# Hybrid attention encoder on one core: attention units started at other places, a second direct weight group, four buffers for weight parts

## Chip, core and metric

The kernel runs on one core of one Trainium2 chip. TensorE (PE) multiplies, VectorE (DVE) and ScalarE (ACT) do the elementwise work, GpSimd (POOL) takes a little of it, and SyncE (SP) issues all transfers. The metric is the device time of one execution in microseconds (us); less is better.

## What is computed

One layer of an encoder is applied to two requests with the same weights: a prompt of 512 tokens and a sample of 1,024 tokens, 1,024 channels each, in float32.

```python
h = rms_norm(x, g_norm)
u = h @ w_in                                   # 1024 x 9728
qa, ka, va, za, qb, kb, vb, zb, qc, kc, vc, zc, gl = jnp.split(u, offs, axis=-1)
ya = neighborhood_attention(qa, ka, va, rpb)   # 8 heads, 8 x 16 window on a grid 64 wide
yb = diff_attention(qb, kb, vb, lam, ...)      # 4 heads, two softmax maps over all keys
yc = dilated_attention(qc, kc, vc, ...)        # 3 groups x 4 heads, windows 128/512/2048
pa = (ya * silu(za)) @ w_br_a                  # pb and pc likewise
merged = gates[:, :, 0] * pa + gates[:, :, 1] * pb + gates[:, :, 2] * pc
y = rms_norm(x + merged @ w_out, g_final)
```

## The kernel before

**Projection.** `w_in` has 9,728 columns, taken 256 at a time: 38 slots for the prompt, then 38 for the sample. A pair of 128 columns is multiplied by the Strassen scheme in `strassen`: seven products of half the inner length instead of eight. Weights and activations are each split into a high part in the fast float32 form and a low part, and a product is three runs of matmuls (`mm3`): high by high, low by high (`wl`), and bfloat16 by low (`wb`). `split_w` makes `wh`, `wl` and `wb` of one weight tile on ACT, DVE and POOL. A prompt matmul has 256 columns, a sample matmul 512. With `direct` the pair is multiplied without sums of weights (`ws`), by eight products. Before the change that holds for the first prompt slot alone (`DIRECT = 1`). Three slots of each request are taken double ("quads", `strassen_v`), for the values.

**Attention units.** Each request has 12 units: four differential heads (`mixer_b`), two pairs of a dilated unit and a window unit (`dilated`, `mixer_c`), and four neighbourhood units (`mixer_a`). All 24 run inside the sample's 38 slots: the prompt's while the first slots are multiplied, the sample's after that. `P_AT` and `S_AT` say at which slot each unit starts; it is spread evenly to the start of the next. A unit begins with a head: it fetches q and k and splits them into high and low halves (`qk<-stg`). A sample unit of `mixer_b` then has 32 softmax rows: one DVE instruction that takes a 128 x 512 tile of scores `s`, adds the distance term in `tab` and finds the maximum. The exponential follows on ACT, a scaled subtraction of the two maps on DVE, transposes on PE with a high and a low copy (`pt`, `pl`), and the product with the values (`o`).

**Order.** Nothing runs by program order alone. Each operation is recorded with a price and its predecessors, and a list scheduler (`Program.order`) decides once, at build time, in which order each engine's instructions stand and which buffer each tile gets. On the chip an engine takes its instructions strictly in that order. `CAPS` limits how many tiles of a name may be alive: `wh` 3, `wl` 2, `wb` 3 before. Operations with two possible engines go to the one that the planner finds less loaded. The priority is the order of recording, so a unit's head goes ahead of later projection work.

**End.** After slot 37 the branch projections and gates follow (`merge`, first prompt, then sample), and the output projection with the last norm (`output`).

The lines that the change touches are the tables after line 500, `CAPS`, and the `direct` branch of `strassen`. Slots are started in this loop:

```python
starts = P_AT + S_AT + [38]
...
        while j < len(units) and slot > starts[j]:
            unit, n = units[j]
            want = int(min(1, (slot - starts[j]) / (starts[j + 1] - starts[j])) * n + 1e-6)
```

Of the kernel before, what the change touches and what calls it, by code (L numbers as in the profile page):

```python
# [8 lines left out]
F32 = mybir.dt.float32  # L9
# [136 lines left out]
class Program:  # L146
# [323 lines left out]
    def emit(self, pools, static_pool, dram_pool):  # L470
# [29 lines left out]


HS_AT = 10
DIRECT = 1
QUADS_P = [2, 5, 8]
QUADS_S = [0, 2, 5]
P_AT = [1.0, 2.25, 3.0, 4.25, 5.0, 6.0, 7.25, 7.75, 8.2, 10.0, 12.25, 13.5]
P_ORDER = [0, 1, 2, 3, 4, 5, 6, 7, 8, 9, 10, 11]
S_AT = [14.2, 17.0, 19.0, 21.0, 23.5, 26.5, 27.0, 27.75, 31.0, 33.0, 34.0, 35.5]
S_ORDER = [0, 1, 2, 3, 4, 5, 6, 7, 8, 9, 11, 10]

SLOTS = {"k9": (2, 9216), "k8": (11, 8192), "k4": (18, 4096), "k2": (18, 2048), "k1": (3, 1024), "b": (8, 2048)}
CAPS = {"tab": ("k9", 2), "x": ("k9", 1), "ybl": ("k9", 1), "tpl": ("k9", 1),
# [7 lines left out]
for _t, (_n, _w) in {"rstd": (2, 1), "ss": (2, 1), "ss2": (3, 2), "st": (4, 4), "cz": (4, 2), "stb": (4, 6),  # L520
                     "czb": (2, 12), "st2": (2, 32), "s2n": (2, 32), "st1": (2, 32), "cmb": (1, 96),
                     "ff": (1, 32)}.items():
    SLOTS["s_" + _t] = (_n, 4 * _w)
    CAPS[_t] = ("s_" + _t, _n)
# [5 lines left out]
def build(ctx, tc, a):  # L530
    nc = tc.nc
    pg = Program(tc, nc, SLOTS, CAPS)
    act, dve, pool, pe = pg.act, pg.dve, pg.pool, pg.pe
# [15 lines left out]
    def copy(dst, src, scale=None, engines="AD"):  # L549

        ways = []
        if "A" in engines:
            ways.append((act, "activation", (dst, src, AF.Copy), {} if scale is None else {"scale": scale}))
        if "D" in engines and scale is None:
            ways.append((dve, "tensor_copy", (dst, src), {}))
        elif "D" in engines:
            ways.append((dve, "tensor_scalar", (dst, src, scale, None), {"op0": OP.mult}))
        pg.any(*ways)
# [73 lines left out]
    def put(dst, src, t):  # L632

        c = slice(128 * t, 128 * t + 128)
        hi, lo = dst
        if isinstance(lo, list):
            for i in range(2):
                split(hi[:, 2 * i:2 * i + 2, c], lo[i][:, :, c], src[:, 2 * i:2 * i + 2])
        else:
            split(hi[:, :, c], lo[:, :, c], src)  # L640
# [94 lines left out]
    def split_w(raw, half=True):  # L735

        n = raw.ap.ap[1][1]
        wh = pg.tile("wh", [128, 4, 128], F32R)[:, :n]
        wl = pg.tile("wl", [128, 4, 128], F32R)[:, :n]
        split(wh, wl, raw)  # L740
        ws = [wh, wl, wh]
        if half:
            ws[2] = pg.tile("wb", [128, 4, 128], BF16)[:, :n]
            copy(ws[2], raw)
        return [[w[:, k] for k in range(n)] for w in ws]

    def mm3(ps, w, xh, xl, first=True):

        n = len(xh)
        kw = {} if first else {"skip_group_check": True}  # L750
        for k in range(n):
            pe.matmul(ps, w[0][k], xh[k], start=first and k == 0, stop=False, **kw)
        for k in range(n):
            pe.matmul(ps, w[1][k], xh[k], start=False, stop=False, **kw)
        for k in range(n):
            pe.matmul(ps, w[2][k], xl[k], start=False, stop=k == n - 1, **kw)

    def strassen(raw, T, n, put, direct=False, early=None):

        a0, a1 = (raw[k][:, :, :128] for k in range(2))  # L760
        b0, b1 = (raw[k][:, :, 128:] for k in range(2))
        if direct:
            for i, (w0, w1) in enumerate(((a0, a1), (b0, b1))):
                w = [x + y for x, y in zip(split_w(w0), split_w(w1))]
                c = pg.tile("c", [128, 512], F32)
                for j in range(2):
                    ps = pg.tile("p", [128, 512], F32)[:, :n]
                    mm3(ps, w, *[[T[f"b{k // 4}{j}"][x][:, k % 4] for k in range(8)] for x in range(2)])
                    copy(c[:, n * j:n * j + n], ps)
                put(i, 0, c)  # L770
                yield
            return

        def ws(x, y, op):
# [813 lines left out]
    T = next(part)  # L1588
# [30 lines left out]
    def slots(s, T):  # L1619

        def make(i):
            quad = i in quads[s]

            def go():
                ahead(s, i + 1 + quad)
                if quad:
                    return project_v(s, cols[s][i], raws[s, i], T)
                return project(s, cols[s][i], raws[s, i], T, s == "p" and i < DIRECT)
            return Pair(not quad and not (s == "p" and i < DIRECT), go)
        return chain([None if c is None else make(i) for i, c in enumerate(cols[s])])  # L1630
# [19 lines left out]
    units = mixers("p", 512, P_ORDER) + mixers("s", 1024, S_ORDER)  # L1650
    starts = P_AT + S_AT + [38]
    ahead("s", 0)
    j = done = slot = 0
    for i, k in slots("s", TS):
        slot = i + k / 7
        while j < len(units) and slot > starts[j]:
            unit, n = units[j]
# [6 lines left out]
            j, done = j + 1, 0  # L1664
# [44 lines left out]
```

## Time and profile before

| what | value |
|---|---|
| median of 3 runs | 1871.55 us (1870.59 to 1872.54) |
| the profiled execution, its own time | 1870.9 us |
| its span, first to last instruction | 1869.1 us |
| mean granted TensorE clock | 0.995 |
| busy: PE / PE weight loads / DVE / ACT / POOL | 97 / 78 / 81 / 65 / 18 % |
| prompt slots end, sample slots end | about 415 us, about 1573 us |

Busy is the time in which an engine executed something. Matmuls are pipelined and each record covers its whole passage, so two that overlap leave no gap: a PE that is shown busy need not be at its peak, and waits shorter than a passage (about 0.3 to 0.4 us) do not show as idle time. The two times at the end are read from the first matmul that stands behind the last prompt slot's and the last sample slot's.

### The profile page before, as it was taken

The numbers are of one execution on the slowest core, as the hardware profiler recorded it, in microseconds if no ns is written. First come the engines' busy times: TensorE is split into PE (matmuls) and PEld (weight loads), VectorE is DVE, ScalarE is ACT, GpSimd is POOL, SyncE is SP. The second block draws the span as 40 slices with busy tenths as digits, with TensorE's granted clock in tenths as the row PEclk, the third lists the DMA queues.
The fourth block names the chain that finished last, engine by engine and source line by source line (L and its number), as shares of the span: only waits on it lengthen the run. The fifth ranks groups of instructions, "written<-read, shape, count | busy, mean of one in ns | idle before, by whom it ended". The sixth has DMA issues, their size and how long they took to land.

```text
span 1869.1 us, 32390 instructions
## 1 busy us (share of the span) xinstructions
PE 1811.9 (97%) x11343; PEld 1465.9 (78%) x11436; DVE 1515.3 (81%) x3061; ACT 1217.8 (65%) x2432; POOL 345.0 (18%) x296
## 2 busy tenths in 40 slices
PE   6999999999999999999999999999999999999998
PEld 6999999999989777778777787767777776666776
DVE  8879999997995786788999988578588886866665
ACT  6677878885675665666565657487587776633453
POOL 0000000000000000000000001000001144988874
PEclk9999999999999999999999999999999999999999
DMA  7645555553334454542122325246354557978541
GB/s 230 178 129 192 165 163 175 164 180 124 122 116 144 140 155 148 172 134 95 64 91 74 100 82 162 76 139 181 121 166 143 158 147 260 326 239 255 200 167 68
DMA packets 242336, 287.14 MB, mean 154 GB/s; under 512 B 33182, under 2 KB 168574, under 8 KB 242174
## 3 DMA queue, kind: packets, MB, share of 16 engines
q1 hardware_dynamic: 242174, 285.08, 48.2%
q8 instruction: 90, 1.47, 0.3%
q14 instruction: 72, 0.59, 0.1%
HBM read 203.93 MB, written 81.44 MB: 153 GB/s over the span
## 4 chain that ended last, share of the span: by engine, by line
PE 86%; DVE 6%; ACT 3%; DMA 2%; issue 1%; SPq 1%; POOL 0%; DVEq 0%; POOLq 0%; ACTq 0%
PE p L486 60%; PE s L486 15%; PE o L486 6%; PE t L486 6%; DVE qk L486 2%; SPq L486 1%; ACT qk L486 1%; DVE e L486 1%; DVE tab L486 1%; DMA rawq<-w_in 1%; ACT wh L486 0%; ACT c L486 0%; DVE wl L486 0%; POOL ybl L486 0%; DMA YG<-y 0%
## 5 line engine op out<-in xcount | busy, mean ns | idle before, releaser
L486 PE MATMUL p<-th,wh 128*128 128x512 f32 x1400 | 424.4, 414 | 2.9 <-ACT c L486 2.1
L486 PEld LDWEIGHTS p<-th,wh 128*128 128x128 f32 x1400 | 252.8, 189 | 58.5 <-issue 5.0
L486 PE MATMUL p<-th,wl 128*128 128x512 f32 x1016 | 295.6, 401 | 0.6 <-DVE wl L486 0.6
L486 ACT ACTIVATE wb<-raw 128x512 bf16<-128x512 f32 (+1 forms) x254 | 154.9, 614 | 177.5 <-PE p L486 99.7
L486 ACT ACTIVATE c<-p 128x512 f32<-128x512 f32 (+1 forms) x302 | 150.7, 500 | 111.5 <-PE p L486 104.5
L486 PEld LDWEIGHTS p<-th,wl 128*128 128x128 f32 x1016 | 186.7, 189 | 39.8 <-issue 2.4
L486 PE MATMUL s<-qk 128*128 128x512 f32 (+5 forms) x736 | 191.4, 363 | 7.1 <-DVE qk L486 4.0
L486 DVE TENSOR_TENSOR c<-p,c 128x512 f32<-128x512 f32 (+1 forms) x222 | 126.0, 576 | 84.0 <-PE p L486 44.8
L486 PEld LDWEIGHTS <-wb 128*128 128x128 bf16 x1376 | 107.6, 98 | 109.5 <-issue 50.1
L486 DVE CUSTOM_DVE_ANT_0 e<-s,tab 128x384 f32<-128x384 f32 (+3 forms) x256 | 129.7, 532 | 75.1 <-PE s L486 66.8
L486 DVE TENSOR_TENSOR wl<-ws,wh 128x512 fp32r<-128x512 f32 x252 | 172.9, 690 | 4.5 <-PE p L486 1.7
L486 ACT ACTIVATE pt<-t 128x512 fp32r<-128x512 f32 (+4 forms) x198 | 102.8, 537 | 96.3 <-PE t L486 93.5
L486 PE MATMUL p<-tp,wh 128*128 128x256 f32 x892 | 151.7, 295 | 4.5 <-ACT wh L486 3.7
L486 ACT ACTIVATE wh<-ws 128x512 fp32r<-128x512 f32 x239 | 148.0, 621 | 8.3 <-DVE ws L486 7.5
L486 PE MATMUL p<-tl,wb 128*128 128x512 bf16 x529 | 145.6, 381 | 4.4 <-issue 0.3
L486 PEld LDWEIGHTS s<-qk 128*128 128x128 f32 (+1 forms) x736 | 123.7, 189 | 31.9 <-issue 9.0
L486 ACT ACTIVATE wh<-raw 128x512 fp32r<-128x512 f32 (+1 forms) x224 | 134.5, 606 | 21.1 <-PE p L486 12.9
L486 PE MATMUL p<-tp,wl 128*128 128x256 f32 x892 | 145.2, 285 | 0.4 <-DVE rstd L486 0.2
L486 DVE TENSOR_TENSOR wl<-raw,wh 128x512 fp32r<-128x512 f32 (+1 forms) x201 | 140.6, 704 | 6.0 <-ACT wh L486 4.0
L486 POOL MEMSET qk<- 64x512 f32 (+1 forms) x48 | 37.2, 774 | 563.9 <-PE t L486 152.3
L486 ACT ACTIVATE e<-e,st 128x384 f32<-128x384 f32 (+2 forms) x192 | 105.2, 550 | 39.6 <-DVE st L486 39.1
L486 PE MATMUL p<-wq,th 128*128 128x256 f32 x816 | 128.4, 294 | 0.0
(230 smaller groups left out, 3773.8 us busy)
## 6 DMA issues: line engine op xcount, KB each, us to landing
raw<-w_in SPq DMA_DIRECT2D x140, 512.0 KB
Us<-c SPq DMA_DIRECT2D x128, 256.0 KB
Up<-c SPq DMA_DIRECT2D x64, 256.0 KB
stg<-Us SPq DMA_DIRECT2D x30, 512.0 KB
g<-Us SPq DMA_DIRECT2D x48, 256.0 KB
tab<-E SPq DMA_DIRECT2D x192, 48.0 KB
stp<-Up SPq DMA_DIRECT2D x30, 256.0 KB
YG<-y SPq DMA_DIRECT2D x30, 256.0 KB
```

The source lines that it names most:

```text
L486: getattr(engs[o.eng], o.meth)(*[val(x) for x in o.args], **{k: val(x) for k, x in o.kw.items()})
```

## The change

Four things: the second prompt slot is multiplied directly too; a direct pair is now gone through by token half first (both column blocks on the first half, then both on the second), with its result stored as soon as its second half is there; up to four tiles of `wh`, `wl` and `wb` may be alive; and the starts of the attention units are others. Of the tables the sample's is shown. The prompt's first five units started at 1.0, 2.25, 3.0, 4.25 and 5.0 and now start at 1.0, 2.4, 3.8, 5.2 and 6.6; the rest follow at distances of 0.8 to 1.0, where they were 0.45 to 2.25.

```diff
-DIRECT = 1
+DIRECT = 2
...
-S_AT = [14.2, 17.0, 19.0, 21.0, 23.5, 26.5, 27.0, 27.75, 31.0, 33.0, 34.0, 35.5]
+S_AT = [14.2, 17.3, 20.4, 23.5, 26.6, 28.2, 29.2, 30.8, 31.8, 33.3, 34.8, 36.3]
...
-SLOTS = {"k9": (2, 9216), "k8": (11, 8192), "k4": (18, 4096), "k2": (18, 2048), "k1": (3, 1024), "b": (8, 2048)}
+SLOTS = {"k9": (2, 9216), "k8": (11, 8192), "k4": (18, 4096), "k2": (18, 2048), "k1": (4, 1024), "b": (8, 2048)}
...
-        "tpb": ("k2", 6), "ws": ("k2", 4), "wh": ("k2", 3), "wl": ("k2", 2), "c": ("k2", 7),
+        "tpb": ("k2", 6), "ws": ("k2", 4), "wh": ("k2", 4), "wl": ("k2", 4), "c": ("k2", 7),
...
-        "ycl": ("k2", 3), "yraw": ("k4", 4), "g": ("k2", 6), "fw": ("k2", 4), "wb": ("k1", 3)}
+        "ycl": ("k2", 3), "yraw": ("k4", 4), "g": ("k2", 6), "fw": ("k2", 4), "wb": ("k1", 4)}
...
         if direct:
-            for i, (w0, w1) in enumerate(((a0, a1), (b0, b1))):
-                w = [x + y for x, y in zip(split_w(w0), split_w(w1))]
-                c = pg.tile("c", [128, 512], F32)
-                for j in range(2):
+            w = [[x + y for x, y in zip(split_w(w0), split_w(w1))] for w0, w1 in ((a0, a1), (b0, b1))]
+            c = [pg.tile("c", [128, 512], F32) for _ in range(2)]
+            for j in range(2):
+                for i in range(2):
                     ps = pg.tile("p", [128, 512], F32)[:, :n]
-                    mm3(ps, w, *[[T[f"b{k // 4}{j}"][x][:, k % 4] for k in range(8)] for x in range(2)])
-                    copy(c[:, n * j:n * j + n], ps)
-                put(i, 0, c)
-                yield
+                    mm3(ps, w[i], *[[T[f"b{k // 4}{j}"][x][:, k % 4] for k in range(8)] for x in range(2)])
+                    copy(c[i][:, n * j:n * j + n], ps)
+                    if j:
+                        put(i, 0, c[i])
+                    yield
             return
```

What the planner makes of it is shown at three places, all on DVE, on which PE waits there.

The first place is the start, where activations and the first weights are prepared (`wl` is the low part of a weight tile, `f` the sums of activations, `tpb` and `tpl` their low parts, `ws` sums of weight tiles). Before:

```order
L486 TENSOR_TENSOR wl<-raw,wh 128x512 x2
L486 TENSOR_TENSOR tpb<-f,tp 128x2x128 x2
L486 TENSOR_TENSOR f<-f 128x512 x2
L486 TENSOR_TENSOR tpl<-f,tp 128x4x128
L486 TENSOR_TENSOR f<-f 128x512 x2
L486 TENSOR_TENSOR wl<-raw,wh 128x512
L486 TENSOR_TENSOR tpb<-f,tp 128x2x128 x2
L486 TENSOR_TENSOR tpl<-f,tp 128x4x128 x2
L486 TENSOR_TENSOR f<-f 128x512
L486 TENSOR_TENSOR ws<-raw 128x512
L486 TENSOR_TENSOR ws<-ws,raw 128x512
```

Now:

```order
L486 TENSOR_TENSOR wl<-raw,wh 128x512
L486 CAST wb<-raw 128x512
L486 TENSOR_TENSOR wl<-raw,wh 128x512
L486 TENSOR_TENSOR tpl<-f,tp 128x4x128
L486 TENSOR_TENSOR tpb<-f,tp 128x2x128 x2
L486 TENSOR_TENSOR wl<-raw,wh 128x512 x2
L486 TENSOR_TENSOR f<-f 128x512 x2
L486 TENSOR_TENSOR tpl<-f,tp 128x4x128
L486 TENSOR_TENSOR tpb<-f,tp 128x4x128
L486 TENSOR_TENSOR f<-f 128x512
```

Four low parts of raw weights stand here where sums of weights (`ws`) followed; the sums now begin with those of the third slot.

The second place is in the sample's differential units, where the head of the next unit (`qk<-stg`) comes in between the rows of the last one (before: in slot 19; now: in slot 20). Before:

```order
L486 ISA tab,stb<-s,tab,stb 128x512
L486 ISA stb 128x1
L486 SCALAR_TENSOR_TENSOR qk<-stg,qk 64x1024 x2
L486 RECIPROCAL czb<-stb 128x1
L486 CAST qk<-stg 64x1024
L486 RECIPROCAL czb<-stb 128x1
L486 SCALAR_TENSOR_TENSOR czb<-stb,czb,neglam 128x1
L486 SCALAR_TENSOR_TENSOR tab<-tab,czb 128x1024
L486 TENSOR_TENSOR qk<-stg,qk 64x1024 x2
L486 TENSOR_TENSOR pl<-t,pt 128x512
L486 TENSOR_TENSOR wl<-ws,wh 128x512
```

Now:

```order
L486 ISA tab,stb<-s,tab,stb 128x512
L486 ISA stb 128x1
L486 TENSOR_TENSOR wl<-raw,wh 128x512 x2
L486 SCALAR_TENSOR_TENSOR qk<-stg,qk 64x1024
L486 RECIPROCAL czb<-stb 128x1 x2
L486 SCALAR_TENSOR_TENSOR czb<-stb,czb,neglam 128x1
L486 SCALAR_TENSOR_TENSOR tab<-tab,czb 128x1024
L486 SCALAR_TENSOR_TENSOR qk<-stg,qk 64x1024
L486 CAST pt<-t 128x512
L486 TENSOR_TENSOR pl<-t,pt 128x512
L486 TENSOR_TENSOR c<-p,c 128x512 x2
```

One long split instead of three stands ahead of the scaled subtraction (`tab<-tab,czb`) that PE's transposes need, and two low weight parts stand ahead of both.

The third place is the start of sample slot 27. Before:

```order
L486 TENSOR_TENSOR wl<-ws,wh 128x512
L486 CAST qk<-stg 64x1024
L486 TENSOR_TENSOR qk<-stg,qk 64x1024 x2
L486 ISA e,st_15467<-s,tab 128x192
L486 ISA st_15467 128x1
L486 ISA e,st_15467<-s,tab 128x256
L486 ISA st_15467 128x1
L486 TENSOR_TENSOR c<-p,c 128x512
L486 ISA e,st_15467<-s,tab 128x192
L486 ISA st_15467 128x1
L486 ISA e,st_15467<-s,tab 128x256
L486 ISA st_15467 128x1
```

Now:

```order
L486 CAST qk<-stg 64x1024
L486 TENSOR_TENSOR ws<-raw 128x512
L486 RECIPROCAL czb<-stb 128x1
L486 SCALAR_TENSOR_TENSOR czb<-stb,czb,neglam 128x1
L486 SCALAR_TENSOR_TENSOR tab<-tab,czb 128x1024
L486 TENSOR_TENSOR qk<-stg,qk 64x1024 x2
L486 TENSOR_TENSOR pl<-t,pt 128x512
L486 TENSOR_TENSOR c<-p,c 128x512
L486 TENSOR_TENSOR wl<-ws,wh 128x512
L486 TENSOR_TENSOR pl<-t,pt 128x512
```

Before, a window unit's softmax rows (192 and 256 columns) and the next dilated unit's head share the slot; now it holds the end of the last differential unit and the first dilated unit's head.

## Rows read from the trace of the kernel before

**Rows 1.** The page's first part: busy time, share, instructions of each engine.

```profile
PE 1811.9 (97%) x11343; PEld 1465.9 (78%) x11436; DVE 1515.3 (81%) x3061; ACT 1217.8 (65%) x2432; POOL 345.0 (18%) x296
```

**Rows 2.** Stages: length; PE, PEld, DVE, ACT, POOL busy; clock, DMA share, GB/s.

```profile
150.00:400.00 250.00, 249.42 (x2103) 241.00 (x2102) 235.67 (x435) 205.05 (x417) 5.25 (x6) 1.00 0.52 167
415.00:456.00 41.00, 41.00 (x344) 39.06 (x342) 28.02 (x52) 19.82 (x37) 0.00 (x0) 1.00 0.44 145
456.00:547.00 91.00, 90.81 (x641) 80.64 (x642) 83.22 (x200) 62.56 (x129) 7.54 (x12) 1.00 0.37 116
547.00:782.00 235.00, 231.72 (x1441) 181.34 (x1456) 172.79 (x417) 147.40 (x319) 10.10 (x18) 1.00 0.50 150
...
782.00:1106.00 324.00, 312.32 (x1670) 247.14 (x1689) 295.93 (x640) 198.25 (x340) 18.08 (x20) 0.99 0.29 93
...
782.00:1217.00 435.00, 418.81 (x2278) 328.47 (x2305) 374.67 (x800) 266.63 (x459) 24.43 (x26) 0.99 0.31 98
1217.00:1573.00 356.00, 347.63 (x2110) 258.32 (x2132) 277.78 (x641) 261.22 (x557) 55.70 (x39) 1.00 0.52 158
1573.00:1869.00 296.00, 283.18 (x1245) 195.71 (x1265) 203.57 (x266) 137.01 (x285) 234.45 (x180) 1.00 0.64 216
```

**Rows 3.** The chain of waits: PE alone, 256 columns, then 512.

```profile
139.08 61.52 PE p L486 x520
...
703.29 11.30 PE p L486 x49
```

**Rows 4.** The timeline of PE around 1224 us: transposes, half-array matmuls.

```profile
1223.23 0.49 PE L486 MATMUL t<-ident,e 128*128 128x128 f32 x3
1223.56 0.38 PE L486 MATMUL p<-tl,wb 128*128 128x512 bf16 x1
...
1226.60 0.88 PE L486 MATMUL o<-pt,v 128*64 128x128 f32 x12
1227.40 0.33 PE L486 MATMUL t<-ident,stg 128*128 128x128 f32 x1
```

**Rows 5.** What PE waited for, 415 to 1573 us: total us, times, longest.

```profile
PE t L486 <- DVE tab L486: 6.9, 6, 2.6
PE s L486 <- DVE qk L486: 4.0, 5, 1.9
```

**Rows 6.** DVE's timeline at the handover to the third differential unit.

```profile
963.17 2.47 DVE L486 SCALAR_TENSOR_TENSOR qk<-stg,qk 64x1024 fp32r<-64x1024 f32 x2
...
965.86 1.33 DVE L486 CAST qk<-stg 64x1024 fp32r<-64x1024 f32 x1
...
967.67 1.28 DVE L486 SCALAR_TENSOR_TENSOR tab<-tab,czb 128x1024 f32<-128x1024 f32 x1
968.88 2.46 DVE L486 TENSOR_TENSOR qk<-stg,qk 64x1024 fp32r<-64x1024 f32 x2
```

**Rows 7.** PE's timeline at the same place.

```profile
969.01 1.11 PE L486 MATMUL t<-ident,tab 128*128 128x128 f32 x4 [2.57 <-DVE tab L486]
```

**Rows 8.** Short stretches around three such waits, columns as in rows 2.

```profile
960.00:970.00 10.00, 7.43 (x39) 5.85 (x38) 9.77 (x17) 7.76 (x11) 1.90 (x2) 0.94 0.55 170
970.00:980.00 10.00, 9.83 (x54) 8.21 (x55) 9.23 (x16) 4.88 (x9) 0.00 (x0) 0.88 0.00 1
1040.00:1050.00 10.00, 7.36 (x41) 5.78 (x39) 9.77 (x18) 7.99 (x11) 1.90 (x2) 1.00 0.57 176
1050.00:1060.00 10.00, 9.32 (x49) 7.86 (x50) 8.49 (x15) 3.90 (x8) 0.00 (x0) 0.83 0.00 0
1255.00:1260.00 5.00, 4.48 (x15) 3.17 (x16) 4.83 (x11) 4.98 (x4) 0.00 (x0) 0.66 0.39 105
```

**Rows 9.** PE's timeline at the second prompt slot's start.

```profile
35.53 0.74 PE L486 MATMUL p<-tp,wh 128*128 128x256 f32 x4 [1.48 <-ACT wh L486]
36.75 0.98 PE L486 MATMUL p<-tp,wh 128*128 128x256 f32 x4 [0.48 <-ACT wh L486]
```

**Rows 10.** ACT's longest waits, over the whole span.

```profile
ACT wb L486 <- PE p L486: 153.5, 153, 3.9
```

More of the change, by code (lines that the diff above doesn't have):

```diff
@@ L502 @@
 HS_AT = 10
-DIRECT = 1
+DIRECT = 2
 QUADS_P = [2, 5, 8]
 QUADS_S = [0, 2, 5]
-P_AT = [1.0, 2.25, 3.0, 4.25, 5.0, 6.0, 7.25, 7.75, 8.2, 10.0, 12.25, 13.5]
+P_AT = [1.0, 2.4, 3.8, 5.2, 6.6, 7.6, 8.4, 9.4, 10.2, 11.2, 12.2, 13.2]
 P_ORDER = [0, 1, 2, 3, 4, 5, 6, 7, 8, 9, 10, 11]
-S_AT = [14.2, 17.0, 19.0, 21.0, 23.5, 26.5, 27.0, 27.75, 31.0, 33.0, 34.0, 35.5]
+S_AT = [14.2, 17.3, 20.4, 23.5, 26.6, 28.2, 29.2, 30.8, 31.8, 33.3, 34.8, 36.3]
 S_ORDER = [0, 1, 2, 3, 4, 5, 6, 7, 8, 9, 11, 10]
-SLOTS = {"k9": (2, 9216), "k8": (11, 8192), "k4": (18, 4096), "k2": (18, 2048), "k1": (3, 1024), "b": (8, 2048)}
+SLOTS = {"k9": (2, 9216), "k8": (11, 8192), "k4": (18, 4096), "k2": (18, 2048), "k1": (4, 1024), "b": (8, 2048)}
 CAPS = {"tab": ("k9", 2), "x": ("k9", 1), "ybl": ("k9", 1), "tpl": ("k9", 1),
```

## The prediction

> **What bounds the kernel now.** The page's first part [rows 1] has PE busy for 97% of the span, DVE for 81%. That alone would say that only PE's own work counts. But matmul records overlap, so I read the stages next [rows 2]. In the prompt's slots (150 to 400) PE runs 2,103 matmuls in 250 us with 0.6 us idle, although DVE is 94% busy there: nothing to gain. In the first sample slots (415 to 456, no attention) it is the same. From 547 on PE has gaps: 3.3 us idle in 547 to 782, 16.2 in 782 to 1217 (sample's differential units), 8.4 in 1217 to 1573 (the other sample units); with the 0.2 of 456 to 547 that makes 28.1 us in the sample's 38 slots. The reader should see that a full DVE is not by itself the cause: in 456 to 547 DVE is 91% busy and PE idles 0.2 us; in 782 to 1106 it is 91% again, and PE idles 11.7.
>
> How much is hidden behind the overlap? Matmuls of 256 columns follow each other at 61.52/520 = 0.118 us, those of 512 at 11.30/49 = 0.231 [rows 3], transposes at (1223.56 - 1223.23)/3 = 0.11, half-array matmuls at (1227.40 - 1226.60)/12 = 0.067 [rows 4]. In the sample's slots stand, by the order, 3,007 of 512 columns, 1,681 of 256, 124 of 384, some 900 of 128 or fewer and 936 half-array ones: 695 + 198 + 22 + 99 + 63 = about 1,077 us, of 1,158 that the slots take. So some 80 us are lost there, 28 of them visible as idle, the others as many short waits and changes of kind.
>
> What ends the visible waits: DVE's scaled subtraction (`tab`, 6.9 us in six) and head splits (`qk`, 4.0 in five) lead the list [rows 5]. One of them can be read line by line. At 963 DVE spends 2.47 and 1.33 us on the next unit's head, and only then, at 967.67, does the subtraction [rows 6]; PE, which takes its queue in order, stands 2.57 us before the transposes of that tile [rows 7], with projection work queued behind them. DVE is 98% busy in that stretch (9.77 of 10). So the loss is a clump on DVE at a unit's handover.
>
> [...] Their price is 10 x (0.06 + 0.12 + 0.17) + 5 x 0.34 = 5.2 us. [...]
>
> **The change, part by part.** *Start.* The second prompt slot by eight products instead of seven has 96 matmuls instead of 84: 12 x 0.118 = +1.4 us on PE. It takes away the sums of weights that PE waited for: 1.48 + 0.48 = 2.0 us [rows 9]. DVE's four low parts of raw weights stand where the sums stood. The next sums, for the third slot, have 192 direct matmuls (23 us) as cover; without it the same 2 us return there. I take -0.6, bounds +1.4 and -2.6 (the wait gone, the added work in gaps of the first 50 us).
>
> *Where DVE's work goes.* A slot costs DVE 28.02/2 = 14.0 us without attention. Slots 14 to 22 (782 to 1106) hold 116 softmax rows by the order, so a row with all that belongs to it costs (295.93 - 9 x 14.0)/116 = 1.46 us. PE needs 20.5 us for a slot (41/2), and per row two matmuls of 512 columns, two transposes, three of 256: 0.46 + 0.22 + 0.35 = 1.03. DVE overtakes PE above 6.5/0.43 = 15 rows. Slots 15 to 23 had 10, 15, 11, 18, 15, 17, 12, 16, 12; now 15 to 26 have 12, 12, 8, 12, 12, 8, 8, 12, 12, 8, 12, 12. Over whole slots the surplus before was only 0.43 x (2.9 + 1.9 + 0.9) = 2.4 us. The rest of the 16.2 idle us is inside slots: handovers. There the order shows one split where three stood ahead of the subtraction, and two `wl` made beforehand: about 1.2 + 1.3 us of DVE ahead of it instead of 3.8, so a wait of 2.57 shrinks by about half. I take 10 of the 16.2, surplus included; bounds 0 and 16.
>
> *Slots 27 to 37.* Slot 27 had 26 softmax rows of window and dilated units and holds ten now; the largest count of these is 18 instead, in slot 31. But this stage also takes over work: the units that began at 23.5 now begin at 26.6, and slots 33 to 37 hold 56 rows of 384 columns where they held 50. DVE has 78% here (277.78 of 356). I take half of the 8.4 idle us, 4; bounds +8 (as much idle again as now, at the crowded end) and -8.
>
> *Slots 2 to 13.* The prompt's differential units go from three and a half slots to five and a half, six rows a slot for 12, 4, 12 before. They lost only 0.2 us; the 3.3 behind them are the prompt's other units, spread more evenly now. I take 1.5; bounds 0 and 3.5.
>
> *Clock.* Fewer long gaps, fewer falls: two thirds of 5.2, 3.5; bounds 0 and 5.
>
> *Hidden waits.* 80 less 28 less 5 is 47 us. Most are changes of kind on PE, which remain: the same units are interleaved with the same products. I take 4, near the lower end; bounds 0 and 22 (half).
>
> *Buffers.* ACT waits 153.5 us for PE to let go of `wb` [rows 10], the longest wait of any engine that feeds PE. With four it waits later and less. ACT has 65%, so this costs nothing as long as the weights are there in time. Their worth is as a reserve: two low parts cover 2 products, 2 x 12 x 0.231 = 5.5 us of a DVE that is busy with a head (6.3 us in the splits shown); four cover 11. That is in the terms above and not counted again. *Merge and output* (1573 to 1869): same instructions, 0; bounds 2 either way.
>
> **Sum.** -0.6 - 10 - 4 - 1.5 - 3.5 - 4 = -23.6, from the profiled 1870.9: 1847.3. The median is 0.65 above that execution: about 1847 to 1848; I say 1847.
>
> [...] The count of matmuls at their measured pitch allows 80 in all 38 slots, and the sum above goes by that.
>
> **Rivals.** *More (1826):* all 28 idle us and 4 of the clock go, and a quarter of the hidden waits (12), since many of these are DVE results a few tenths late: -45. For it: in the prompt's slots, with even work, the loss is nil. Against: sample slots mix four kinds of matmul.
>
> *Little (about 1863):* clumps are moved, not dissolved. Two thirds of the forecast gain are given back at the crowded end (slots 33 to 37, where a neighbourhood unit now has 1.5 slots and its two score tables wait for the two `tab` buffers): -8.
>
> *Nothing (1871):* PE's 1,077 us of work and its changes of kind are the bound and the waits only change place.
>
> *Slower (about 1893):* handovers become the rule. DVE is now nearly full from slot 2 to 37, with no emptier stretch (1217 to 1573 was one) in which it catches up. If every one of the sample's 12 handovers cost what the one at 966 did, 2.57 idle and 1.8 of clock, that is 52 us against 28 + 5 now, and the rest of the schedule gains nothing: +19 to +22. It decides from the eighth handover on (8 x 4.4 = 35). Against it: the order at the second place shows fewer splits in a row; at the third place two are still in a row.
>
> **How the numbers follow.** A measurement of this kernel tells about 0.2% (4 us) from no change. Forecast (1835 to 1858): 0.48. More (below 1835): 0.15. Little (1858 to 1868): 0.18. Nothing (within 0.2%): 0.07. Slower: 0.12. So faster 0.81, same 0.07, slower 0.12. The range goes from 1822, which leaves out a part of "more", to 1872, which leaves out "slower".
>
> **What would show it.** Right: in the stage of the sample's differential units PE idles under 2% with the clock at 1.00 throughout; `tab` and `qk` fall in PE's list of waits; the second prompt slot follows the first without a wait for `wh`; DVE's share in 782 to 1217 and 1217 to 1573 comes closer together. Wrong: waits of 2 to 3 us on `tab`, `e` or `qk` in slots 27 to 37, or a fall of the clock there; PE waiting for `wl` or `wh` in the third prompt slot; a longer merge because the last neighbourhood units end late.

## The result and the profile after

The changed kernel takes 1845.44 us (median of 4, 1845.30 to 1846.71), the one before 1871.53 (median of 4, 1870.59 to 1872.54): a ratio of 0.9859, 95% interval 0.9844 to 0.9873, or -26 us. The profiled execution spans 1843.8 us, 25.3 less than the 1869.1 of before, at a mean granted clock of 0.996 (0.995).

The page's first part of the changed kernel, which answers to [rows 1]:

```profile
PE 1802.0 (98%) x11353; PEld 1466.4 (80%) x11448; DVE 1546.3 (84%) x3081; ACT 1209.4 (66%) x2411; POOL 328.1 (18%) x284
```

DVE is busy for 31 us more in a shorter span, and PE loses less. Where, the stages of the changed kernel say (columns as in [rows 2]; the edges are moved to the same slots, but the sample's differential units now reach to 1170):

```profile
150.00:400.00 250.00, 249.14 (x2106) 241.05 (x2106) 237.94 (x436) 203.97 (x416) 5.31 (x6) 1.00 0.52 169
408.00:449.00 41.00, 41.00 (x345) 39.12 (x342) 28.21 (x52) 21.71 (x40) 0.00 (x0) 1.00 0.43 144
449.00:775.00 326.00, 324.13 (x2095) 262.80 (x2111) 260.61 (x624) 207.20 (x445) 17.48 (x30) 1.00 0.44 133
775.00:1140.00 365.00, 362.85 (x1918) 288.48 (x1941) 327.24 (x692) 224.73 (x382) 17.66 (x22) 1.00 0.32 106
1140.00:1170.00 30.00, 29.86 (x155) 23.78 (x156) 26.51 (x56) 18.95 (x29) 1.45 (x2) 1.00 0.33 100
1170.00:1548.00 378.00, 366.30 (x2305) 275.86 (x2331) 305.17 (x705) 281.03 (x594) 50.70 (x36) 0.99 0.52 157
1548.00:1844.00 296.00, 283.13 (x1240) 196.08 (x1261) 226.53 (x274) 136.87 (x281) 227.84 (x174) 0.99 0.65 216
```

In the differential units PE now idles 2.15 + 0.14 = 2.3 us in 395 (0.6%) at a clock of 1.00, where it idled 16.2 in 435 [rows 2], although DVE's share has hardly changed (89.7% in 775 to 1140, 91% in 782 to 1106 before). The stage behind it idles more than before, 11.7 us against 8.4, because it took work over and because the last differential handover falls into it (below).

Step by step, in both traces. The planner lets a few matmuls of the next slot run ahead (four of the third prompt slot before 46.7 us in the kernel before), so an edge is counted off: it is the start of the matmul that comes next when as many have started as the slots ahead of it hold.

| stretch | before, us | after, us | difference |
|---|---|---|---|
| start to the third prompt slot | 46.7 | 41.9 | -4.8 |
| prompt slots 2 to 37 | 368.8 | 366.9 | -1.9 |
| sample slots 0 and 1 | 40.7 | 40.4 | -0.3 |
| sample slots 2 to 13 | 326.1 | 325.9 | -0.2 |
| sample slots 14 to 37 | 791.0 | 773.2 | -17.8 |
| merge and output | 295.8 | 295.5 | -0.3 |

The sum is -25.3. The 17.8 are 10.6 of visible idle time (16.2 + 8.4 against 2.15 + 0.14 + 11.7), some 1.8 of clock (5.2 against the 3.4 shown below) and a rest of 5.4 that no idle time shows.

What PE waits for in 408 to 1548 in the changed kernel, as [rows 5]:

```profile
PE s L486 <- DVE qk L486: 2.2, 4, 0.8
PE t L486 <- DVE tab L486: 1.9, 1, 1.9
PE t L486 <- DVE e L486: 1.8, 3, 0.9
PE s L486 <- ACT qk L486: 1.4, 1, 1.4
```

`tab` falls from 6.9 us in six waits to a single one, `qk` from 4.0 to 2.2. The single one left is the handover from the last differential unit to the first dilated one. PE's timeline there (waits in brackets):

```profile
1173.94 0.35 PE L486 MATMUL s<-qk 128*128 128x256 f32 x1 [0.74 <-DVE qk L486]
1176.22 0.66 PE L486 MATMUL t<-ident,tab 128*128 128x128 f32 x4 [1.93 <-DVE tab L486]
1178.27 0.58 PE L486 MATMUL s<-qk 128*128 128x256 f32 x1 [1.40 <-ACT qk L486]
```

DVE's timeline beside it:

```profile
1172.76 1.03 DVE L486 CAST qk<-stg 64x1024 fp32r<-64x1024 f32 x1
...
1174.88 1.28 DVE L486 SCALAR_TENSOR_TENSOR tab<-tab,czb 128x1024 f32<-128x1024 f32 x1
1176.08 3.84 DVE L486 TENSOR_TENSOR qk<-stg,qk 64x1024 fp32r<-64x1024 f32 x2
```

And the windows of the same place (columns as in [rows 2], clock third from the end):

```profile
1170.00:1180.00 10.00, 5.87 (x24) 3.59 (x22) 9.14 (x11) 9.93 (x12) 0.95 (x1) 0.85 0.59 228
1180.00:1190.00 10.00, 10.00 (x54) 8.78 (x53) 8.05 (x16) 5.74 (x8) 0.00 (x0) 0.81 0.42 131
```

It reads like [rows 6 and 7]: a head's split, then the subtraction, and PE stands 1.93 us with its queue behind the transposes. The price is 4.1 us of idle time and 1.5 + 1.9 = 3.4 us of clock; in the sample's slots this is the only fall of the clock left. A new one stands behind them: 1550 to 1560, in the merge, is at 0.83, which is 1.7 us.

The start, in windows (same columns). First the kernel before:

```profile
20.00:30.00 10.00, 9.59 (x71) 9.10 (x72) 9.48 (x18) 7.76 (x17) 0.00 (x0) 0.83 1.01 276
30.00:35.00 5.00, 4.05 (x35) 3.58 (x34) 4.78 (x9) 3.89 (x10) 0.00 (x0) 1.00 0.88 276
35.00:40.00 5.00, 3.82 (x18) 3.33 (x19) 4.66 (x8) 4.34 (x8) 0.00 (x0) 0.71 0.06 22
40.00:45.00 5.00, 5.00 (x42) 4.92 (x42) 4.53 (x10) 2.44 (x5) 0.00 (x0) 0.95 0.05 14
0.00:50.00 50.00, 35.19 (x241) 32.05 (x241) 41.49 (x78) 34.94 (x71) 4.22 (x10) 0.93 0.71 225
```

Then the changed kernel:

```profile
20.00:30.00 10.00, 9.71 (x84) 9.12 (x84) 9.58 (x19) 8.88 (x20) 0.00 (x0) 1.00 0.94 268
...
0.00:50.00 50.00, 37.56 (x292) 34.94 (x293) 40.70 (x76) 35.89 (x74) 4.38 (x10) 1.00 0.71 229
```

The clock's falls cost the start of before 10 x 0.17 + 5 x 0.29 + 5 x 0.05 = 3.4 us, that of after nothing. The two waits of [rows 9] are gone.

### The profile page after: what moved, and what is told of

It is laid out like the page before. It is cut to its first block, busy times and chain, and to the rows that moved or that the text cites. A ratio compares the mean times of both kernels' runs of the same rounds, so it can differ in the third digit from the quotient of the medians.

```text
span 1843.8 us, 32386 instructions
## 1 busy us (share of the span) xinstructions
PE 1802.0 (98%) x11353; PEld 1466.4 (80%) x11448; DVE 1546.3 (84%) x3081; ACT 1209.4 (66%) x2411; POOL 328.1 (18%) x284
## 4 chain that ended last, share of the span: by engine, by line
PE 93%; DVE 3%; ACT 2%; issue 1%; DMA 0%; SPq 0%; POOL 0%; DVEq 0%; POOLq 0%; ACTq 0%
PE p L486 64%; PE s L486 16%; PE o L486 6%; PE t L486 6%; ACT qk L486 1%; DVE qk L486 1%; DVE e L486 0%; ACT c L486 0%; DMA xp<-x_prompt 0%; DVE wl L486 0%; DVE c L486 0%; DVE tab L486 0%; DVE ws L486 0%; DVE xt L486 0%; ACT tab L486 0%
## 5 line engine op out<-in xcount | busy, mean ns | idle before, releaser
L486 ACT ACTIVATE c<-p 128x512 f32<-128x512 f32 (+1 forms) x291 | 144.8, 498 | 125.4 <-PE p L486 122.3
L486 PE MATMUL s<-qk 128*128 128x512 f32 (+5 forms) x736 | 186.9, 361 | 4.7 <-DVE qk L486 2.2
L486 DVE TENSOR_TENSOR wl<-ws,wh 128x512 fp32r<-128x512 f32 x251 | 179.1, 716 | 11.8 <-ACT wh L486 6.5
L486 ACT ACTIVATE pt<-t 128x512 fp32r<-128x512 f32 (+3 forms) x193 | 100.7, 539 | 101.3 <-PE t L486 99.1
L486 DVE TENSOR_TENSOR wl<-raw,wh 128x512 fp32r<-128x512 f32 x212 | 155.6, 746 | 6.1 <-ACT wh L486 2.6
L486 ACT ACTIVATE wh<-ws 128x512 fp32r<-128x512 f32 x240 | 147.7, 621 | 13.4 <-DVE ws L486 10.6
L486 PE MATMUL p<-tp,wh 128*128 128x256 f32 x888 | 147.2, 294 | 2.4 <-ACT wh L486 2.4
L486 PE MATMUL p<-wq,th 128*128 128x256 f32 x816 | 124.6, 292 | 0.0
```

What stands on the lines that cost most here:

```text
L486: getattr(engs[o.eng], o.meth)(*[val(x) for x in o.args], **{k: val(x) for k, x in o.kw.items()})
```

## The experiments

The kernel before was timed beside each group of runs, at 1871.6 to 1872.3 us. "Start times" are `P_AT` and `S_AT`, "buffers" the four tiles each of `wh`, `wl` and `wb`, "direct" the new branch with `DIRECT = 2`. The first six runs complete all eight combinations of the three. Every time is the median of a run's executions; stage lengths, waits and clocks come from one profiled execution, whose own time is given where it lies far from the median. The planner lays out each of these programs anew, so a run changes the order of instructions along with the part that it names.

**Runs 1 to 3: the change with one part undone.** The start times of before:

```diff
-S_AT = [14.2, 17.3, 20.4, 23.5, 26.6, 28.2, 29.2, 30.8, 31.8, 33.3, 34.8, 36.3]
+S_AT = [14.2, 17.0, 19.0, 21.0, 23.5, 26.5, 27.0, 27.75, 31.0, 33.0, 34.0, 35.5]
```

(and `P_AT` likewise).

> The changed kernel with the old starts of the attention units (prompt and sample); direct second slot and four buffers stay. Leaves nothing out. Theory A (spacing gives the gain in the sample's slots, because VectorE's clumps at handovers thin out): 18 us of the 26 come back, about 1863, with PE's waits of 2 to 3 us on tab and the falls of the clock around them in the differential units' stage. Theory B (the deeper weight buffers give it): about 1848, the stage as good as in the changed kernel.

Measured: 1871.24 us, ratio 0.9995 [0.9985, 1.0004]. All of the gain is gone: without the spacing the other two parts together give nothing. What PE waits for in its sample slots, 409 to 1578:

```profile
PE t L486 <- DVE tab L486: 9.1, 6, 3.4
PE s L486 <- DVE qk L486: 4.0, 5, 1.4
```

The list of before is back: six waits for `tab`, as in [rows 5]. The third prompt slot starts at 42.7 us, early as in the changed kernel; the 4 us won there are lost again in the sample's slots, which take 1168.0 us (1157.8 before, 1139.5 after). The profiled execution took 1876.6 us, 5 more than the median, so about half of the 10 us over the kernel before is its own.

The buffers of before:

```diff
-        "tpb": ("k2", 6), "ws": ("k2", 4), "wh": ("k2", 4), "wl": ("k2", 4), "c": ("k2", 7),
+        "tpb": ("k2", 6), "ws": ("k2", 4), "wh": ("k2", 3), "wl": ("k2", 2), "c": ("k2", 7),
```

(`wb` back to 3 and its memory likewise).

> The changed kernel with 3 wh, 2 wl and 3 wb buffers as before; starts and direct slots as changed. Theory A (spacing): 1846 to 1848, at most 2 us for the buffers. Theory B (buffers as a reserve while VectorE is busy with a head): 1855 to 1863, PE idle in the differential units' stage over 8 us instead of 2.

Measured: 1859.26 us, 0.9925 [0.9909, 0.9940], 13.8 more than with the buffers; the profiled execution spans 15.4 more. By the starts of the stages 1.5 us of it stand before the third prompt slot, 1.6 in the other prompt slots, 4 in the first 34 sample slots (without more idle time), 7 in the last four, 1.8 behind them. The last four slots of this kernel, in windows:

```profile
1424.00:1562.00 138.00, 132.76 (x821) 99.68 (x818) 109.09 (x263) 99.54 (x218) 30.76 (x20) 0.98 0.54 162
```

The changed kernel:

```profile
1417.00:1548.00 131.00, 129.55 (x815) 98.37 (x824) 108.73 (x271) 96.30 (x212) 29.57 (x19) 1.00 0.57 171
```

PE idles 5.2 us against 1.5, and the clock costs some 2.8. In this window PE waits 4.0 us for `e` in three waits and once 1.1 us for `wl`, a low weight part that was not made ahead. So the time is theory B's, but its sign did not come: in the differential units (778 to 1176) PE idles 2.5 us, hardly more than the 2.3 of the changed kernel, and nothing like 8.

The direct branch and `DIRECT = 1` of before:

```diff
-DIRECT = 2
+DIRECT = 1
...
-            for j in range(2):
-                for i in range(2):
+            for i, (w0, w1) in enumerate(((a0, a1), (b0, b1))):
...
+                for j in range(2):
```

> The changed kernel with one direct prompt slot, multiplied by column block first as before; starts and buffers as changed. If the start's gain is the wait for sums of weights and the fall of the clock behind it, 5 to 7 us come back: about 1851, clock of the first 50 us 0.93 again, second slot 14 us long. If the start's gain came from elsewhere (other order of loads, buffers): 1845 to 1847.

Measured: 1849.30 us, 0.9872 [0.9858, 0.9887], 3.9 more. The third prompt slot starts at 46.7 us again, against 41.9, with the clock of the first 50 us at 0.93. The intervals of this run and of the changed kernel overlap a little, their executions do not (1848.37 and up against 1846.71 and less). The direct pair is thus worth its start and no more.

**Runs 4 to 6: the kernel before with one part.** The edits are those of the change, one at a time.

> The kernel before with the new starts alone. Theory A: the 18 us of the sample's slots are there without the rest, about 1853. Theory B: nothing without the buffers, 1868 to 1872. If both are needed together: 1862 or so.

Measured: 1863.97 us (1858.94 to 1867.62), 0.9949 [0.9930, 0.9968], 8 us less. What PE waits for in 410 to 1570 (the profiled execution took 1867.62):

```profile
PE t L486 <- DVE e L486: 7.1, 7, 2.2
PE s L486 <- DVE qk L486: 3.1, 4, 1.2
```

`tab` is gone from the list, `e` now leads it. The sample's slots hold 19.1 us of idle time, nearer to the 15.9 of the changed kernel than to the 28.0 of before, and 5.1 of clock. Yet they take about 1152 us, where the changed kernel takes 1139.5 and the kernel before 1157.8: the start times alone bring 8.9 of the 12.1 us of visible idle time that the whole change brings there, and a third of the time.

> The kernel before with four wh, wl and wb buffers alone. If buffers and spacing work only together (a reserve helps only where VectorE gets ahead again between two clumps): 1868 to 1874, with the differential units' stage and its falls of the clock as before. If buffers are worth 13 us by themselves: about 1858.

Measured: 1875.04 us, 1.0019 [1.0009, 1.0029], 3 us more. The prompt slots win 2 (366.5 us against 368.8), the sample's slots lose 10 (1167.8 against 1157.8) in the profiled execution, which took 1879.55 us; at the median, 4.5 us lower, some 5 are left of the 10.

> The kernel before with the second direct slot by token half first alone. The start's theory (wait for sums of weights, and the clock behind it): the third prompt slot begins 4 to 5 us earlier, clock of the first 50 us near 1.00, about 1867. If the sample's slots hand it back: 1871.

Measured: 1870.54 us, 0.9991 [0.9982, 1.0001]. The third prompt slot starts 3.5 us earlier (43.2), the first sample slot 3.8 earlier (411.7), and the merge 1.1 later (1574.4): given back in the sample's slots, 5.1 us of it by the clock (10.2 lost there, 5.1 before). The profiled execution took 1873.67 us, 3 more than the median, so the median run gives back less.

The eight together:

| start times | buffers | direct | us |
|---|---|---|---|
| old | old | old | 1871.5 to 1872.3 |
| old | old | new | 1870.54 |
| old | new | old | 1875.04 |
| old | new | new | 1871.24 |
| new | old | old | 1863.97 |
| new | old | new | 1859.26 |
| new | new | old | 1849.30 |
| new | new | new | 1845.44 |

The table is not a sum of three effects. Buffers cost up to 3 us under the old start times (3 without the direct pair; the 0.7 with it are not clear of the spread) and bring 14 to 15 under the new ones; the start times bring 8 to 11 without the buffers and 26 with them. The direct pair brings 4 to 5, and 1 to 2 in the kernel before, where the interval reaches 1.

**Run 7: spacing by time alone.** The sample's units keep their first and last places, but the starts are equally far apart.

```diff
-S_AT = [14.2, 17.3, 20.4, 23.5, 26.6, 28.2, 29.2, 30.8, 31.8, 33.3, 34.8, 36.3]
+S_AT = [14.2, 16.18, 18.17, 20.15, 22.13, 24.12, 26.1, 28.08, 30.07, 32.05, 34.03, 36.02]
```

> The changed kernel with the sample's 12 units at equal distances of 1.98 slots instead of distances by VectorE's work; the differential units then have 15 to 17 softmax rows a slot. If the load of VectorE in each slot decides (more than 15 rows: VectorE overtakes PE): the differential stage loses 12 us or more against the changed kernel and the later stage wins some 5 back, 1852 to 1858. If any even spacing without packed slots is enough: 1845.

Measured: 1882.42 us, 1.0056 [1.0039, 1.0073], 37 more than the changed kernel and 11 more than before. A differential unit has 32 softmax rows and now gets two slots instead of three: slots 14 to 22 hold 12, 15, 15, 17, 15, 17, 15, 17 and 14 rows. Its stages (columns as in [rows 2]):

```profile
776.00:1009.00 233.00, 222.71 (x1185) 176.16 (x1197) 210.62 (x461) 145.59 (x250) 12.92 (x16) 0.97 0.30 100
1009.00:1170.00 161.00, 150.60 (x834) 117.84 (x841) 133.84 (x282) 105.06 (x176) 8.72 (x11) 0.96 0.31 102
```

What PE waits for in 408 to 1585:

```profile
PE t L486 <- DVE tab L486: 10.4, 7, 3.1
PE t L486 <- DVE cz L486: 3.9, 2, 3.7
```

20.7 us of idle time in 394, and the clock at 0.97 and 0.96, some 13 us: the waits are paid in idle time and again in clock. The time is 24 us above the upper end of the first forecast. This is the rival "slower" of the prediction. Equal distances are not what the change does; it gives each unit slots by its rows.

**Run 8: how many low parts.** The changed kernel with two `wl` (`"wl": ("k2", 2)`), `wh` and `wb` at four.

> The changed kernel with two wl buffers as before, but four wh and four wb. If the reserve against VectorE's clumps is the low parts that VectorE itself makes: most of the 14 us that the old buffers cost comes back, 1855 to 1860, PE idle at the end of the sample's slots over 4 us. If wh or wb was the tight one (ScalarE's wait for PE to let go of wb): 1846 to 1849.

Measured: 1852.61 us, 0.9898 [0.9883, 0.9913], 7.2 more, between the two forecasts. In the last four slots (1420 to 1556) PE idles 6.6 us against 1.5, as the first theory has it. So about half of the buffers' 13.8 goes with `wl`, and half with the fourth `wh` and `wb`, if the halves add up; nearly half of DVE's instructions stand in another order than in the changed kernel.

**Run 9: the order of the halves.** The changed kernel with both direct pairs by column block first, as the direct branch of before:

```diff
-            for j in range(2):
-                for i in range(2):
+            for i, (w0, w1) in enumerate(((a0, a1), (b0, b1))):
+                w = [x + y for x, y in zip(split_w(w0), split_w(w1))]
+                c = pg.tile("c", [128, 512], F32)
+                for j in range(2):
```

> The changed kernel, with both groups of the first projection direct, but each group finishes one half of the columns (both token halves) before the other and stores both halves in one go, as in the kernel before. Theory A (the gain at the start is the absence of the weight sums and of the clock fall that their waits bring; the order of the halves is worth nothing): the third prompt slot begins at 41 to 43 us and the clock up to 50 us is 0.99 or more, 1844 to 1848. Theory B (token half first is what keeps PE fed while the second half's tokens still arrive): the third prompt slot begins 1.5 to 4 us later, with PE waits for tp or tl in the first 30 us, 1847 to 1851.

Measured: 1847.47 us (1847.23 to 1850.98), 0.9869 [0.9850, 0.9887], 2.0 more; the intervals overlap. The third prompt slot starts at 44.3 us, 2.4 later. No wait for `tp` or `tl` stands in the first 45 us, so the reason that theory B gave is not there; the clock is. Its window of 20 to 30:

```profile
20.00:30.00 10.00, 9.23 (x67) 8.53 (x66) 9.42 (x17) 8.31 (x17) 0.00 (x0) 0.83 0.99 277
```

0.83 again, 1.7 us. Whether the order of the halves or a small shift of the waits before 20 us brings that fall stays open. The order alone does not decide it: runs 4 and 5 go by column block too and stand at 1.00 in this window, run 1 goes by token half and stands at 0.89.

**Run 10: the last clump, moved.** The first dilated unit's start goes from 26.6 to 26.2, so that its head stands earlier.

> The changed kernel with one starting time altered: the first dilated unit begins at 26.2 instead of 26.6. Theory (a clump at a handover costs its idle time and the clock fall behind it, and goes away when the two heads stand apart): in 1165 to 1195 PE's idle time falls from 4.1 us to under 2, the clock there is 1.00 (1.5 and 1.9 us lost in the two stretches now), and the time falls by 3 to 7 us, to 1838 to 1842. Rival (a clump only changes its place; which place is luck of the order): the idle time of 1170 to 1190 shows up elsewhere in the sample's slots, 1843 to 1850.

Measured: 1848.15 us (1847.24 to 1848.32), 0.9865 [0.9852, 0.9879], 2.7 more, which these intervals do not tell from the changed kernel; the 3 to 7 us less did not come, and the theory failed. The wait for `tab` at 1176 is gone, and another has taken its place. PE's timeline:

```profile
1169.76 0.80 PE L486 MATMUL o<-pt,v 128*128 128x256 f32 x2 [4.00 <-ACT pt L486]
```

This stretch loses 4.6 us in 1165 to 1195, after 4.2 in the changed kernel, with a clock of 0.89 in both. Moving this start by 0.4 slots did not dissolve the clump; another copy came last.

**Runs 11 and 12: POOL's fills.** Run 2 left a question: what makes `e` late in the last slots? There one split of 64x512 on DVE took 3.27 us that takes 0.42 in the mean of the changed kernel, beside a fill of a neighbourhood unit's score table on POOL. In run 11 each of the eight fills is done twice; the second writes the same values.

```diff
                 pool.memset(t_, -8 * BIG)
+                pool.memset(t_, -8 * BIG)
```

> The changed kernel with each of the eight fills of a neighbourhood unit's score table (2.03 us on POOL, 128x2304) done twice. Theory (while POOL writes to SBUF, DVE's one-input forms from SBUF to SBUF, the splits, copies and scalings, stand until POOL is done, as one of 0.42 us that took 3.27; two-input forms of 0.68 us do not): one-input DVE instructions that begin in the second fill end with it, at 1 to 4 us instead of 0.3 to 0.7, DVE's time over the usual durations rises by 8 to 16 us in 1300 to 1548, PE idles 1 to 5 us more there, 1846 to 1851. Rival (the long ones are long by themselves, whatever POOL does): DVE's excess and the time are unchanged, 1844 to 1847.

Measured: 1859.94 us, 0.9930 [0.9917, 0.9942], 14.5 more than the changed kernel, far above the range that I had given the theory. POOL's timeline at two of the units' heads:

```profile
1402.34 8.24 POOL L486 MEMSET tab<- 128x2304 f32 x4 [41.31 <-DVE st L486]
```

DVE's beside it:

```profile
1402.62 0.69 DVE L486 TENSOR_TENSOR ws<-raw,ws 128x512 f32<-128x512 f32 x1
...
1403.69 0.68 DVE L486 TENSOR_TENSOR wl<-ws,wh 128x512 fp32r<-128x512 f32 x1
...
1404.48 4.14 DVE L486 TENSOR_SCALAR e<-e,cz 128x384 f32<-128x384 f32 x1
...
1408.72 2.07 DVE L486 TENSOR_SCALAR e<-e,cz 128x384 f32<-128x384 f32 x1
```

And PE's:

```profile
1408.67 0.55 PE L486 MATMUL t<-ident,e 128*128 128x128 f32 x3 [2.40 <-DVE e L486]
1410.84 0.90 PE L486 MATMUL t<-ident,e 128*128 128x128 f32 x3 [1.39 <-DVE e L486]
```

The scaling `e<-e,cz` takes 0.42 us elsewhere. It begins beside the second fill and ends behind the third; the next one ends with the fourth fill (1402.34 + 8.24 = 1410.58). Two-input instructions beside the same fills take 0.68 and 0.69, as the medians of the same instructions in the changed kernel (0.685 and 0.684). PE's queue stands behind the transposes of `e` for 2.40 and 1.39 us. Behind the first of the extra fills the planner's order differs from the changed kernel's too, so a part of the 14.5 us may be that order.

In run 12 the fill is cut to the columns that the loads do not cover for every row, in two pieces.

```diff
-                pool.memset(t_, -8 * BIG)
+                tv = t_[:, :2304].rearrange("p (s c k) -> p s c k", s=2, c=3)
+                pool.memset(tv[:, :, :, :128], -8 * BIG)
+                pool.memset(tv[:, :, :, 256:], -8 * BIG)
```

> The changed kernel with the fill of a neighbourhood unit's score table cut to the columns that no load covers for all rows: two pieces of 768 elements in place of one of 2304 (some 0.7 us each, 1.36 instead of 2.03 us of POOL a fill, eight fills). Nothing else of the computation changes. Theory (POOL's fills hold up DVE's one-input forms; a second fill of 2.03 us cost 14.5 us over eight): taking away a third of the fills, and letting DVE in between the two pieces, gives back 3 to 8 us: long one-input instructions of DVE beside fills fall to 1.4 us and less, 1837 to 1842. Rival (what doubling costs does not come back when halving, since PE hardly waits there now, 0.3 us on e from 1417 on): 1843.5 to 1847.

Measured: 1844.16 us (1843.23 to 1844.48), 0.9851 [0.9837, 0.9864], 1.3 less than the changed kernel and not to be told from it by these intervals. The window 1300 to 1548 of the changed kernel:

```profile
1300.00:1548.00 248.00, 243.77 (x1531) 183.74 (x1550) 205.90 (x496) 183.96 (x400) 44.02 (x29) 1.00 0.54 159
```

Of run 11, fills twice:

```profile
1300.00:1548.00 248.00, 235.01 (x1415) 175.32 (x1431) 203.84 (x467) 176.47 (x378) 62.45 (x38) 0.97 0.48 142
```

Of run 12, fills shortened:

```profile
1300.00:1548.00 248.00, 244.19 (x1535) 184.10 (x1552) 199.77 (x495) 185.59 (x402) 39.43 (x38) 1.00 0.54 158
```

Doubled, the fills cost PE 8.8 us more idle time (13.0 against 4.2) and 0.03 x 248 = 7.4 of clock. Shortened, they give DVE back 6.1 us and PE only 0.4. So the blocked DVE time is real in the changed kernel too, but PE idles little for it there: 1.8 us for `e` in three waits. What about 2 us of a held-up scaling cost PE differs: no idle time at 1501.86 in the changed kernel (1.95 us; PE has other matmuls until the transposes at 1503.87), 0.95 us at 1396.90 (2.18 us) and 1.39 in run 11 (2.07 us at 1408.72), where the transposes stood for it.

## Why the prediction was right, and where it was not

Forecast 1847, measured 1845.44; the sign, the range and the main mechanism, DVE's clumps at the handovers, held. That the sum came within 2 us is partly luck: the start and the prompt's slots gave 6.1 us more than their terms (-6.7 against -0.6), the sample's slots 4.7 less (-18.3 against -23).

- **Differential units and slots 27 to 37** (-10 and -4): visible idle time fell by 10.6 us in both together. In the first stage it fell by 13.9 (16.2 to 2.3), more than the 10 taken, inside the bound of 16; in the second it rose by 3.3 where 4 less were expected, inside the bounds of 8. The last differential unit ends three slots later now and takes its handover into the second stage, so the two stages should have been one term.
- **The 15 rows.** That DVE overtakes PE above 15 softmax rows a slot fits what was measured: with 12 or fewer rows PE idles 0.6%, with 14 to 17 in most slots (run 7) 4.4 and 6.5%. As a price it fails. Two rows above 15 in each of three slots are 0.43 x 6 = 2.6 us, and run 7 costs 37 more than the changed kernel. By PE's list of waits (`tab`, `cz`) the price is that of the handovers, which find no room on DVE when the slots around them are full.
- **Clock** (-3.5): the sample's part fell by 1.8 only, since the handover at 1176 kept its fall. The 5.2 us that the term starts from are what the clock column of [rows 8] lacks to 1.00. Read us by us, that column is at 1.00 or 0.50 in both traces, with values between them only where a fall begins or ends: 969 to 972 stand at 0.50 in the kernel before, behind the wait of 2.57 us, and 973 to 977 at 1.00. Such a fall comes to 3.4 us at 0.50, the one at 1177 in the changed kernel to 6.8; those at the spans' ends are not counted here. The prediction counted the falls of the sample's slots alone; over the whole span, the falls at the start, in the merge and at the end included, the clock cost 9.8 us before and 7.4 now.
- **Hidden waits** (-4): the rest that neither idle time nor clock shows is 5.4. Its size is near, its place was not foreseen: by runs 2 and 4 it comes with the buffers (below).
- **Start** (-0.6, bounds +1.4 and -2.6): this term failed; -4.8 was measured, outside its bounds. The step that failed is "takes away the sums of weights that PE waited for: 1.48 + 0.48 = 2.0 us": it priced the waits and not the clock that fell beside them. A window of the first 50 us would have shown 0.93 and 3.4 us; +1.4 of work, 2.4 less of idle time and these 3.4 make -4.4. PE is slow in a stretch ahead of these falls too: in both kernels the first three groups of eight transposes (8.6 to 16.6 us) take 1.97 us each, as long as the one at 20.41 in the kernel before, where the column reads 0.50, and the one at 20.62 in the changed kernel takes 1.07. The column reads 1.00 in the first 20 us and does not show this; what sets it, no run shows. It is the same in both kernels and not in the 3.4. The falls that make up the 3.4 stand behind it, among the start's waits, in a stretch with 15 us of PE idle time. But the idle time of a stretch does not tell whether it falls: 20 to 30 us is at 0.83 with 0.41 us idle before, and at 1.00 with 1.72 in run 4.
- **Slots 2 to 13** (-1.5): -0.2. Idle time fell from 3.5 to 1.9, but the stretch is no shorter.
- **Merge** (0): -0.3.
- **Buffers** ("in the terms above and not counted again"): the weakest step, though it did not move the sum. The four buffers are not an extra to the spacing; without them it pays a third. With the prediction's working I would have given run 4, the start times without the buffers, nearly the whole -23; it measured -8, although 8.9 of the 12.1 us of idle time were gone. Of the 10.6 us by which run 2's sample slots are longer than the changed kernel's, idle time shows 1.4 and the clock 1.7; some 7 us are time that shows as neither. That the buffers act as the reserve which the prediction describes is not shown: PE waits for `wl` once in run 2, 1.1 us. The planner's new order is a rival that the runs leave standing. Besides, the buffers bring 2 us in the prompt's slots (366.5 to 366.9 us with them, 368.8 without), where the prediction saw "nothing to gain", since PE idles only 0.6 us there.

Of the signs named ahead, these came: PE idle under 2% in the differential units, `tab` and `qk` down, the second prompt slot without a wait for `wh` (from 30.71 to 41.89 us PE has no gap). One did not: DVE's share in the two stages, 86 and 78% before [rows 2], is 90 and 81% now, no closer together. And one sign of "wrong" did appear, the waits and the clock fall at 1170 to 1190. It cost 7.5 us and was outweighed.

The rivals: "slower" exists (run 7), but needs full slots at the handovers. The crowded end of "little" shows up without the buffers (run 2: 5.2 us of idle time in the last four slots) and not with them (1.5). "Nothing" is what the change gives without its start times (run 1). For "more" PE would have had to lose nothing: 15.9 us of idle time are left in the sample's 38 slots.

Open: why four buffers cost some 5 us in the sample's slots under the old start times (run 5). In the profiled execution the clock takes 6.8 us more there than before (11.9 against 5.1) and idle time 6.6 more, 4 of them in the last four slots; whether the buffers do this or only the planner's new order, the runs don't separate. The same holds for what the buffers bring under the new start times (runs 2 and 8). Nor do they tell how much of the 7 us that run 2 loses in its last four slots belongs to the missing buffers and how much to the place where a fill on POOL now fell.

## What to carry to other kernels

Where attention work is laid between the matmuls of a projection, give each unit slots by its work on the fullest engine, and look at what stands in that engine's order where one unit ends and the next begins: the waits that showed here stood there (`tab` 6.9 us, `qk` 4.0), and the average share did not tell of them. They are not all of the loss: time that no idle time shows changed by several us from run to run here. Try a schedule and the depth of the buffers that feed it together: alone they gave 8 us less and 3 us more here, together 23 less. Read the granted clock over the start as over the rest (its falls cost 3.4 us in the first 50 us here), and price a wait with the fall of the clock that stands beside it.

## What the runs showed of the hardware

POOL's fills held up DVE here. In three cases a cast or a scaling on DVE from SBUF to SBUF that began beside a MEMSET on POOL ended only 0.1 to 0.3 us behind the end of a fill: a split of 64x512 took 3.27 us in run 2, a scaling of 128x384 4.14 in run 11 and 2.18 in the changed kernel, where 0.42 is usual (the mean of the changed kernel's four such splits, the median of its scalings). One that had begun just before kept its time, and the fill was the longer one: 0.69 us for a cast at 1320.72 in the changed kernel, and 2.58 instead of 2.03 for the fill at 1320.79. The 2.18 us in DVE's timeline of the changed kernel:

```profile
1396.90 2.18 DVE L486 TENSOR_SCALAR e<-e,cz 128x384 f32<-128x384 f32 x1
```

and POOL, whose fill ends at 1398.88, just before that scaling does:

```profile
1396.85 2.03 POOL L486 MEMSET tab<- 128x2304 f32 x1 [33.98 <-DVE st L486]
```

Two-input instructions and those that read PSUM kept their time beside a fill (0.68 and 0.55 in run 11), and so did reciprocals of 128x1 (0.16). Beside TENSOR_TENSOR on POOL some two-input ones took longer: 2.28 us for `wl<-ws,wh` at 1509.08 and 1.67 for `ws<-raw,ws` at 1514.35 in the changed kernel, where the medians are 0.685 and 0.684; and in run 2, where the same took 1.22 at 1427.88 in the kernel before, DVE's timeline has:

```profile
1519.53 3.19 DVE L486 TENSOR_TENSOR qk<-stg,qk 64x1024 fp32r<-64x1024 f32 x1
```

and POOL:

```profile
1519.24 2.39 POOL L486 TENSOR_TENSOR qk<-stg,qk 64x1024 fp32r<-64x1024 f32 x1 [0.77 <-ACT qk L486]
1521.71 2.17 POOL L486 TENSOR_TENSOR wl<-raw,wh 128x512 fp32r<-128x512 f32 x1
```

POOL need not be all of that: the two splits at 1176.08 in the changed kernel took 3.84 us together, and POOL's timeline has nothing beside them. What I had not expected is the price: eight more fills of 2.03 us on an engine that is busy for 18% of the span cost 14.5 us, nearly as much as POOL's added time, since the scaling that waits is the one whose result PE's queue stands for (8.6 us of PE's idle time end with `e` in run 11, 1.8 in the changed kernel); how much of it is the planner's changed order is not separated.
